# First stage of a hybrid retention and latent-attention step: sample latents in plain float32 column groups, gate weights asked for a tile ahead, gate stores asked for by ScalarE

## The chip, the cores and the metric

The kernel runs on one NeuronCore of one Trainium2 chip. The metric is the device time of one execution in microseconds (us). Instructions of TensorE (PE), VectorE (DVE), ScalarE (ACT), GpSimd (POOL) and SyncE (SP) run in five in-order queues, which wait for each other by semaphores. In the before kernel SP asks for nearly all transfers between HBM and on-chip memory.

## The reference

One inference step of a decoder layer in float32, for 1024 prompt rows and 32 sample rows (8 sequences of 4 tokens), each of 1024 features. Cut to what the change touches:

```
z = rmsnorm(x, ln_w) @ w_in
rq, rk, rv, rg, cq, ckv, kr, mg, ga, gb = split(z)
q   = rmsnorm(cq, q_norm_w) @ w_uq        # cq: 384 columns
ckv = rmsnorm(ckv, kv_norm_w)             # 256 columns
kr  = rope(kr, pos)                       # 64 columns
... retention over (rq, rk, rv), gated by silu(rg)
... paged attention of the sample rows over cached ckv and kr, by a page table; causal attention of the prompt rows; gated by silu(mg)
merged = sigmoid(ga) * h_ret + sigmoid(gb) * h_mla
... output projection, a per-layer embedding, a last norm
```

The change concerns the 704 latent columns (cq, ckv, kr) of the input projection, and its gate columns (ga, gb, rg, mg).

## The kernel before

Float32 products are made from fp32r parts: each operand is split into a high part (a rounded copy, made by ACT or POOL) and a low part (operand less high part, by DVE), and a product is three matmuls, high by high, high by low, low by high (`mac`, L266 to L268). Weights come in by `load_w` and `stage`: SP loads a 128x512 piece into `wr` (two buffers), POOL makes `wh` (L197; later ACT does, L247), DVE makes `wl` (L200).

The first stage treats x in nine tiles in the order `[0, 1, 8, 2, 3, 4, 5, 6, 7]`; tile 8 holds the 32 sample rows. `turn_tile` makes the squares of a tile on ACT (L348, into `xs`), the row norm (`rs_v`, `rs_r`, L233 and L235) on POOL, the transposes on PE (L323, eight of 128x128), copies of them (L324), and stores the turned tile to `xTD`. `scale_tile` spreads the norm over partitions by a matmul (L356), multiplies on DVE (L359, `y`), and makes `xh` on ACT (L364) and `xl` on DVE (L365) for each of eight k blocks. `latent_tile` multiplies a tile by the latent weights (`load_lat`: raw `wlr`, parts `wlh` and `wll`, eight k blocks of 704 columns): 24 matmuls of 384 columns and 24 of 320, whatever the number of rows. Then, twice, squares on ACT (L399), a norm on POOL, a scaling on DVE (L401), the rotation on DVE (L375 to L380), stores, and for prompt rows a block transpose (`lt`, L331) with stores to `latD`. The sample rows' latents stay in `latS`, which `sample_queries` transposes next (L507).

`gate_tiles` is the fill: each gate tile loads one weight tile of 128 columns and runs three thirds of 24 matmuls with 352 columns into one of two `mm` banks; ACT evicts each into `gev` (L417) and SP stores it (L418). `beside` runs the latents of the last three tiles, the sample queries and the page attention with units of that fill between them; what is left runs after. `page_rows` works out the row numbers of the cache pages from the page table; its two tiles, `pt_all` and `own`, lie in the two `xs` buffers. Inside these streams a scheduler places the instructions of each engine, by its own estimates; the order on each engine is then fixed.

## Time and profile before

| | |
|---|---|
| time, three runs | 2135.68, 2136.15, 2139.07 us; median 2136.15 |
| the profiled execution | 2134.45 us; span from first to last instruction 2132.7 |
| granted TensorE clock, mean | 0.998 |
| busy: PE, DVE, ACT, POOL | 2096.1, 1262.0, 723.8, 329.7 us |
| DMA | 316.31 MB, 148 GB/s over the span |

The profile is of one execution. In a timeline a row has the start, the length, the engine, the line, the operation, the tiles written and read, how many are grouped in it, and in square brackets the idle time before it with what ended that. Matmuls are pipelined: a row's length is longer than the step to the next one. SPq rows are the asking for a transfer, not the transfer. In a chain of waits "x <- y: a, b, c" reads: x waited for y, a us in all, b times, the longest c. Names carry no buffer numbers in the profile; in the order of instructions below they do.

### The profile page before, as it was taken

How to read it: one execution, taken by the hardware profiler on the slowest of the kernel's cores; microseconds unless marked ns; L12 is line 12 of the kernel's file. 1: busy time of each engine (PE TensorE's matmuls, PEld its weight loads, DVE VectorE, ACT ScalarE, POOL GpSimd, SP SyncE). 2: the span in 40 equal slices, each digit the busy share in tenths (PEclk: the TensorE clock that was granted, in tenths of full speed). 3: DMA queues.
4: the chain of work that ended last, by engine and by line, in shares of the span. 5: the costliest groups of instructions: out<-in, count | busy, mean ns of one | idle time of the engine just before them, and what ended most of it. 6: DMA issues, size and time to landing. Idle time of an engine off the chain costs nothing. (4 is left out here: it accounts for less than half of the span.)

```text
span 2132.7 us, 38999 instructions
## 1 busy us (share of the span) xinstructions
PE 2096.1 (98%) x15392; PEld 1840.9 (86%) x15392; DVE 1262.0 (59%) x2849; ACT 723.8 (34%) x1541; POOL 329.7 (15%) x522
## 2 busy tenths in 40 slices
PE   8999999999999999999999999999999999999998
PEld 7998777777778897888888887888888999999997
DVE  6535555565655457767676774877777353444465
ACT  5412222333423322222222222454565341222343
POOL 2110111111100022222222220122211000000122
PEclk9999999999999999999999999999999999999999
DMA  7476656566565332754636647210112452333243
GB/s 215 121 218 232 233 192 237 207 246 228 194 237 183 112 75 71 220 147 139 220 72 182 189 139 254 55 46 18 39 56 91 138 192 81 101 87 121 82 143 118
DMA packets 330552, 316.31 MB, mean 148 GB/s; under 512 B 92160, under 2 KB 283840, under 8 KB 326272
## 3 DMA queue, kind: packets, MB, share of 16 engines
q1 hardware_dynamic: 321152, 229.92, 35.8%
q0 software_dynamic: 9216, 83.89, 10.5%
q8 instruction: 121, 1.98, 0.4%
q14 instruction: 63, 0.52, 0.1%
HBM read 245.38 MB, written 68.36 MB: 147 GB/s over the span
## 5 line engine op out<-in xcount | busy, mean ns | idle before, releaser
L266 PE MATMUL mm<-xh,wh 128*128 128x352 f32 x1344 | 455.9, 339 | 0.1
L268 PE MATMUL mm<-xh,wl 128*128 128x352 f32 x1344 | 435.6, 324 | 0.6 <-DVE wl L200 0.6
L267 PE MATMUL mm<-xl,wh 128*128 128x352 f32 x1344 | 435.6, 324 | 0.0
L266 PEld LDWEIGHTS mm<-xh,wh 128*128 128x128 f32 x1344 | 252.4, 188 | 83.3 <-issue 73.3
L267 PEld LDWEIGHTS mm<-xl,wh 128*128 128x128 f32 x1344 | 253.6, 189 | 3.5 <-issue 2.3
L268 PEld LDWEIGHTS mm<-xh,wl 128*128 128x128 f32 x1344 | 253.3, 189 | 3.2 <-issue 1.9
L200 DVE TENSOR_TENSOR wl<-wr,wh 128x512 fp32r<-128x512 f32 (+2 forms) x251 | 176.3, 715 | 119.6 <-ACT wh L247 100.8
L247 ACT CAST wh<-wr 128x512 fp32r<-128x512 f32 x216 | 129.8, 618 | 282.5 <-PE mm L267 254.6
L652 DVE STREAM_TRANSPOSE kt<-craw 128x512 f32<-128x512 f32 x256 | 160.7, 680 | 84.5 <-PE sc L656 79.7
L417 ACT ACTIVATE gev<-mm 128x352 f32<-128x352 f32 x120 | 55.5, 463 | 223.5 <-PE mm L268 141.7
L266 PE MATMUL mm<-mh,wh 128*128 128x352 f32 x384 | 124.6, 324 | 1.4 <-ACT mh L1151 0.8
L267 PE MATMUL mm<-ml,wh 128*128 128x352 f32 x384 | 124.9, 325 | 0.7 <-DVE ml L200 0.6
L268 PE MATMUL mm<-mh,wl 128*128 128x352 f32 x384 | 124.4, 324 | 0.0
L268 PE MATMUL mm<-gh,wl 128*128 128x352 f32 x384 | 124.4, 324 | 0.0
L266 PE MATMUL mm<-gh,wh 128*128 128x352 f32 x384 | 124.4, 324 | 0.0
L267 PE MATMUL mm<-gl,wh 128*128 128x352 f32 x384 | 124.3, 324 | 0.0
L266 PE MATMUL mm<-wv,xh 128*128 128x512 f32 x256 | 103.6, 405 | 0.0
L267 PE MATMUL mm<-wv,xh 128*128 128x512 f32 x256 | 101.0, 395 | 0.0
L268 PE MATMUL mm<-wv,xl 128*128 128x512 f32 x256 | 100.9, 394 | 0.0
L656 PE MATMUL sc<-kt,q 32*32 32x512 f32 x2560 | 91.3, 600 | 0.0
L1580 POOL TENSOR_TENSOR xr<-x1h,x1l 128x352 f32<-128x352 f32 x24 | 27.0, 1146 | 389.1 <-DVE pT L200 311.5
L856 ACT ACTIVATE on<-ac,gb,gs 128x512 f32<-128x512 f32 x36 | 28.0, 778 | 155.1 <-DVE gb L854 150.0
(383 smaller groups left out, 4532.0 us busy)
## 6 DMA issues: line engine op xcount, KB each, us to landing
wr<-in_w_in_dram SPq DMA_DIRECT2D x144, 256.0 KB, 3.6
st<-in_state_ret_dram SPq DMA_DIRECT2D x32, 512.0 KB, 5.3
out_ret_sample_dram<-st SPq DMA_DIRECT2D x32, 512.0 KB, 3.9
wr<-in_w_ple_gate_dram SPq DMA_DIRECT2D x48, 256.0 KB, 2.8
gt<-gev SPq DMA_DIRECT2D x48, 176.0 KB, 3.6
gl<-go SPq DMA_DIRECT2D x16, 528.0 KB, 5.2
gate<-ga SPq DMA_DIRECT2D x16, 528.0 KB, 3.5
g<-gt SPq DMA_DIRECT2D x32, 256.0 KB, 3.2
```

What stands on the lines that cost most here:

```text
L200: dve.tensor_tensor(out=out, in0=src, in1=b32(hi), op=ALU.subtract)
L247: hi_by[0](hi, raw)
L266: pe.matmul(out, wh, xh, start=first, stop=False)
L267: pe.matmul(out, wh, xl, start=False, stop=False)
L268: pe.matmul(out, wl, xh, start=False, stop=last)
L417: act.activation(t, ps, func)
L652: dve.transpose(kt[:, 2 * i + s].rearrange("p (n r) -> p n r", r=32), src)
L656: pe.matmul(sc[32 * v:32 * v + 32, q, :], Q["q4"][qs_, j + v // 2, 2 * (g % 2) + v % 2, :], kt[qs_, v, :], start=n == 0, stop=n == NJ // 2 ...
L856: act.activation(on[:n], po, AF.Identity, bias=nb[:n], scale=s[:n])
L1580: pool.tensor_tensor(out=xr, in0=b32(x1[f][0][:, sl]), in1=b32(x1[f][1][:, sl]), op=ALU.add)
```

## The change

The sample rows leave the ring of tiles. Their x is loaded and turned right behind tile 0, the turned blocks are multiplied by the norm weight on POOL (`xS`, L481, in a `gev` buffer), and 32 plain float32 matmuls, four column groups of 176 for each k block, run on the raw weights `wlr` (now five buffers) between the matmuls of tile 0's first half (L395), into an `mm` bank. At tile 8's place in the ring only the copies out of that bank (four on ACT, L412), the scaling by the row norm on DVE (L413) and the norms remain. `la` has three buffers, `xs` one; `page_rows` takes the `wr` buffers and does its arithmetic two tiles later than its load. `gate_tiles` is one generator over all its groups: it asks for the next weight tile at the fourth of a tile's 24 units, and for the first at the third tile of the ring (`next(fill)`); the fifth merge-gate tile is in the fill itself. The gate stores are asked for by ACT (L440). In the last retention head the fill is cut after 36 units instead of 49.

```diff
@@ -305,11 +305,11 @@
 
     def load_lat(k):
         hi, lo = (p1.tile([P, NLAT], F32R, tag=f"wl{s}{k}", name=f"wl{s}{k}", bufs=1) for s in "hl")
-        raw = p1.tile([P, NLAT], F32, tag="wlr", name="wlr", bufs=4)
+        raw = p1.tile([P, NLAT], F32, tag="wlr", name="wlr", bufs=5)
         sp.dma_start(raw, w_in[k * P:(k + 1) * P, C_LAT:C_LAT + NLAT])
         (hi_pool if k % 2 else act.copy)(hi, raw)
         lo_of(lo, raw, hi)
-        wlat.append((hi, lo))
+        wlat.append((hi, lo, raw))
 
     def turn_input(t, src, dst, nf, by=act.copy):
 
@@ -344,9 +344,13 @@
         n = rows(t)
         xt = xts.pop(t)
         ss = small(p1, "ss")
-        xs = p1.tile([P, D], F32, tag="xs", name="xs", bufs=2)
+        xs = p1.tile([P, D], F32, tag="xs", name="xs", bufs=1)
         act.activation(xs[:n], xt[:n], AF.Square, accum_out=ss[:n])
         r = rstd_of(p1, ss, n, 1.0 / D, dve if t == 0 else pool)
+        if t == 8:
+            r8 = small(p1, "r8", 1, 1)
+            pool.tensor_copy(r8[:n], r[:n])
+            r = r8
         turned[t] = r, turn_input(t, xt, xTD, D // P, dve.tensor_copy if t == 0 else act.copy)
 
     def scale_tile(t):
@@ -384,15 +388,31 @@
     latS = lp.tile([NR, NLAT], F32, name="latS")
     idx = lp.tile([P, NB * NPG // 16], I32, name="idx")
 
+    NG = NLAT // 4
+
+    def sample_latents(k):
+        for r in range(4):
+            pe.matmul(few[0][r * NR:(r + 1) * NR, :NG], few[1][:, k], wlat[k][2][:, r * NG:(r + 1) * NG], start=k == 0, stop=k == 7,
+                      tile_position=(0, r * NR), skip_group_check=True)
+
     def latent_tile(t):
         n = rows(t)
-        pq, pk = ac(), ac()
-        for ps, lo, w in ((pq, 0, QL), (pk, QL, KL + ROPE)):
-            for k in range(8):
-                xk = tuple(v[:, t * P:t * P + n] for v in xn[k])
-                wk = tuple(v[:, lo:lo + w] for v in wlat[k])
-                mac(ps[:n, :w], xk, wk, k == 0, k == 7)
-        la = latS if t == 8 else p1.tile([P, NLAT], F32, tag="la", name="la", bufs=2)
+        if t < 8:
+            pq, pk = ac(), ac()
+            for ps, lo, w in ((pq, 0, QL), (pk, QL, KL + ROPE)):
+                for k in range(8):
+                    xk = tuple(v[:, t * P:t * P + n] for v in xn[k])
+                    wk = tuple(v[:, lo:lo + w] for v in wlat[k][:2])
+                    mac(ps[:n, :w], xk, wk, k == 0, k == 7)
+                    if t == 0 and lo == 0:
+                        sample_latents(k)
+        else:
+            raw = p1.tile([NR, NLAT], F32, tag="la", name="las", bufs=3)
+            for r in range(4):
+                act.activation(raw[:, r * NG:(r + 1) * NG], few[0][r * NR:(r + 1) * NR, :NG], AF.Copy)
+            dve.tensor_scalar(raw, raw, few[2][:NR], None, op0=ALU.mult)
+            pq, pk = raw[:, :QL], raw[:, QL:]
+        la = latS if t == 8 else p1.tile([P, NLAT], F32, tag="la", name="la", bufs=3)
         cq, kv, kr = la[:n, 0:QL], la[:n, QL:QL + KL], la[:n, QL + KL:NLAT].unsqueeze(1)
         for src, dst, w, nw in ((pq[:n, :QL], cq, QL, qnw), (pk[:n, :KL], kv, KL, kvw)):
             ss = small(p1, "ss2")
@@ -408,45 +428,59 @@
             sp.dma_start(O["ckv_sample"].rearrange("l b t c -> (l b t) c"), kv)
             sp.dma_start(O["krope_sample"].rearrange("l b t c -> (l b t) c"), la[:n, QL + KL:])
 
-    def gate_tiles(col, dst, fs, func):
-        for f in fs:
-            w = load_w(w_in[:, col + f * P:col + (f + 1) * P], 8)
-
-            def evac(j, ps, sl, f=f):
+    def gate_tiles(*groups):
+        todo = [(w_in[:, col + f * P:col + (f + 1) * P], dst[f], func) for col, dst, fs, func in groups for f in fs]
+        w = load_w(todo[0][0], 8)
+        yield 0.0
+        for n, (_, dst, func) in enumerate(todo):
+
+            def evac(j, ps, sl, dst=dst, func=func):
                 t = wst.tile([P, TH], F32, tag="gev", name="gev", bufs=2)
                 act.activation(t, ps, func)
-                sp.dma_start(dst[f][:, sl], t)
-            yield from gemm(w, xn, evac, 8)
+                act.dma_start(dst[:, sl], t)
+
+            for i, cost in enumerate(gemm(w, xn, evac, 8)):
+                if i == 3 and n + 1 < len(todo):
+                    w = load_w(todo[n + 1][0], 8)
+                yield cost
 
     def chain(*gs):
         for g_ in gs:
             yield from g_
 
-    fill = chain(gate_tiles(C_GA, gaD, range(8), AF.Copy), gate_tiles(C_GB, gbD, range(8), AF.Copy),
-                 gate_tiles(C_RG, [t[:, f, :] for t in gtD for f in range(4)], range(16), AF.Silu), gate_tiles(C_MG, mgD, range(4), AF.Silu))
+    fill = gate_tiles((C_GA, gaD, range(8), AF.Copy), (C_GB, gbD, range(8), AF.Copy),
+                      (C_RG, [t[:, f, :] for t in gtD for f in range(4)], range(16), AF.Silu), (C_MG, mgD, range(5), AF.Silu))
 
     def page_rows():
-        pt_all = p1.tile([P, NB * NPG], I32, tag="xs", name="pt_all", bufs=2)
+        pt_all = wst.tile([P, NB * NPG], I32, tag="wr", name="pt_all", bufs=2)
         sp.dma_start(pt_all, A["page_table"].rearrange("b n -> (b n)").unsqueeze(0).to_broadcast([P, NB * NPG]))
-        own = p1.tile([P, NB * NPG], F32, tag="xs", name="own", bufs=2)
+        yield
+        own = wst.tile([P, NB * NPG], F32, tag="wr", name="own", bufs=2)
         dve.tensor_copy(own, pt_all)
         own = own.rearrange("p (i g) -> p i g", g=16)
         dve.tensor_tensor(out=own, in0=own, in1=C("page").unsqueeze(1).to_broadcast([P, NB * NPG // 16, 16]), op=ALU.mult)
         row = small(p1, "row", NB * NPG // 16, 1)
         dve.tensor_reduce(out=row, in_=own, axis=AX.X, op=ALU.add)
         dve.tensor_scalar(idx, row, C("mod"), None, op0=ALU.add)
+        yield
 
     head = at["maskT"][0]
     load_x(0)
     sp.dma_start(cst[:, :head], A["consts"][:, :head])
     sp.dma_start(lnw, A["ln_w"][0].rearrange("(f p) -> p f", p=P))
+    load_x(8)
     turn_tile(0)
     scale_tile(0)
     order = [0, 1, 8, 2, 3, 4, 5, 6, 7]
-    for k in range(8):
+    load_lat(0)
+    load_x(1)
+    turn_tile(8)
+    few = [mm(), wst.tile([P, 8, NR], F32, tag="gev", name="xS", bufs=2), turned[8][0]]
+    for half, st in enumerate(turned[8][1]):
+        fs = slice(4 * half, 4 * half + 4)
+        pool.tensor_tensor(out=few[1][:, fs], in0=st[:, :, :NR], in1=lnw[:, fs].unsqueeze(2).to_broadcast([P, 4, NR]), op=ALU.mult)
+    for k in range(1, 8):
         load_lat(k)
-        if k % 4 == 0:
-            load_x(order[1 + k // 4])
     sp.dma_start(qnw, A["q_norm_w"][0:1, :].to_broadcast([P, QL]))
     sp.dma_start(kvw, A["kv_norm_w"][0:1, :].to_broadcast([P, KL]))
     sp.dma_start(ropeM, A["ropeM"])
@@ -455,21 +489,22 @@
     load_x(order[3])
 
     def latents():
+        table = page_rows()
         for n, t in enumerate(order):
             if n + 4 < 9:
                 load_x(order[n + 4])
             if 0 < n < 7:
                 turn_tile(order[n + 2])
             latent_tile(t)
-            if n == 0:
-                turn_tile(order[2])
             if n < 7:
                 scale_tile(order[n + 2])
             if n == 1:
                 sp.dma_start(cst[:, head:], A["consts"][:, head:at["turn"][0]])
                 sp.dma_start(gnw, A["ret_gn_w"][0].rearrange("(f p) -> p f", p=P))
-            if n == 4:
-                page_rows()
+            if n in (4, 6):
+                next(table)
+            if n == 2:
+                next(fill)
             yield 7.1 if n > 5 else 0.0
 
     beside(latents(), 3 * 7.1, fill, 36)
@@ -759,7 +794,6 @@
     gph.close()
     open_banks()
     run(fill)
-    run(gate_tiles(C_MG, mgD, range(4, 5), AF.Silu))
     ph.close()
     lph.close()
 
@@ -1124,8 +1158,8 @@
             def early(cost):
                 first_w.extend(rope_weights(0))
                 yield cost
-            gates = gate_tiles(C_MG, mgD, range(5, 8), AF.Silu)
-            rest = (chain(islice(gates, 49), early(0.0), gates), 31.8)
+            gates = gate_tiles((C_MG, mgD, range(5, 8), AF.Silu))
+            rest = (chain(islice(gates, 36), early(0.0), gates), 31.8)
         run(woven((chain(chunks, sample_state(h, X)), 27.9 if h + 1 < HR else 32.4), rest))
         X = nxt
     hi_by[0] = hi_pool
```

**PE at tile 0.** What stood in its row before, from the start of the latents (`xh_112` and `xl_113` to `xh_126` and `xl_127` are the parts of the eight k blocks of the turned x, `wlh` and `wll` those of the weights; L356 is the scale matmul):

```order
L266 MATMUL ac<-wlh_187,xh_112 128x384
L267 MATMUL ac<-wll_188,xh_112 128x384
L266 MATMUL ac<-wlh_187,xh_112 128x320
L267 MATMUL ac<-wll_188,xh_112 128x320
L268 MATMUL ac<-wlh_187,xl_113 128x384
L266 MATMUL ac<-wlh_195,xh_114 128x384
L267 MATMUL ac<-wll_196,xh_114 128x384
L268 MATMUL ac<-wlh_195,xl_115 128x384
L268 MATMUL ac<-wlh_187,xl_113 128x320
```

and now:

```order
L323 MATMUL tr<-cst,xt 128x32 x8
L395 MATMUL mm<-wlr,xS 32x176 x4
L323 MATMUL tr<-cst,xt 128x128 x8
L266 MATMUL ac<-wlh_189,xh_112 128x384
L266 MATMUL ac<-wlh_189,xh_112 128x320
L267 MATMUL ac<-wll_190,xh_112 128x384
L268 MATMUL ac<-wlh_189,xl_113 128x384
L267 MATMUL ac<-wll_190,xh_112 128x320
L268 MATMUL ac<-wlh_189,xl_113 128x320
L360 MATMUL tr<-cst,rs_r_276 128x128
L360 MATMUL tr<-cst,r_204 128x32
L395 MATMUL mm<-wlr,xS 32x176 x4
```

The turned sample tile and its first four float32 matmuls stand ahead of tile 1's transposes and of the first latent; further groups follow between the latents.

**SP at the start.** Before:

```order
L303 DMA xt<-in_x_prompt_dram 128x1024
L441 DMA cst<-in_consts_dram 128x129
L442 DMA lnw<-in_ln_w_dram 128x8x1
L309 DMA wlr<-in_w_in_dram 128x704
L303 DMA xt<-in_x_prompt_dram 128x1024
L309 DMA wlr<-in_w_in_dram 128x704
L325 DMA xTD<-turn 128x4x128 x2
L309 DMA wlr<-in_w_in_dram 128x704 x3
L303 DMA xt<-in_x_sample_dram 32x1024
L309 DMA wlr<-in_w_in_dram 128x704 x3
```

and now:

```order
L303 DMA xt<-in_x_prompt_dram 128x1024
L469 DMA cst<-in_consts_dram 128x129
L470 DMA lnw<-in_ln_w_dram 128x8x1
L303 DMA xt<-in_x_sample_dram 32x1024
L309 DMA wlr<-in_w_in_dram 128x704
L303 DMA xt<-in_x_prompt_dram 128x1024
L325 DMA xTD<-turn 128x4x128 x2
L325 DMA xTD<-turn 128x4x32 x2
L309 DMA wlr<-in_w_in_dram 128x704 x7
```

The sample rows are loaded third, and the second to eighth weight tile stand behind the four stores of turned tiles 0 and 8.

**POOL at the end of the ring.** The last norms of tiles 6 and 7 (two each) and the gate weights, before:

```order
L233 TENSOR_SCALAR rs_v_1354<-ss_1352 128x1
L235 TENSOR_TENSOR rs_r_1356<-rs_v_1354,cst 128x1
L233 TENSOR_SCALAR rs_v_1361<-ss_1359 128x1
L235 TENSOR_TENSOR rs_r_1363<-rs_v_1361,cst 128x1
L197 TENSOR_SCALAR wh<-wr 128x512 x5
L233 TENSOR_SCALAR rs_v_1538<-ss_1536 128x1
L235 TENSOR_TENSOR rs_r_1540<-rs_v_1538,cst 128x1
L197 TENSOR_SCALAR wh<-wr 128x512
L233 TENSOR_SCALAR rs_v_1545<-ss_1543 128x1
L235 TENSOR_TENSOR rs_r_1547<-rs_v_1545,cst 128x1
```

and now:

```order
L233 TENSOR_SCALAR rs_v_1358<-ss_1356 128x1
L235 TENSOR_TENSOR rs_r_1360<-rs_v_1358,cst 128x1
L233 TENSOR_SCALAR rs_v_1365<-ss_1363 128x1
L235 TENSOR_TENSOR rs_r_1367<-rs_v_1365,cst 128x1
L233 TENSOR_SCALAR rs_v_1542<-ss_1540 128x1
L235 TENSOR_TENSOR rs_r_1544<-rs_v_1542,cst 128x1
L233 TENSOR_SCALAR rs_v_1549<-ss_1547 128x1
L235 TENSOR_TENSOR rs_r_1551<-rs_v_1549,cst 128x1
L197 TENSOR_SCALAR wh<-wr 128x512 x6
```

Before, five weight pieces stand ahead of tile 7's norms and one between them; now all six stand behind them.

**PE at the same place.** The last of tile 7's latents (`ac<-`) and what follows (`mm<-` is gate work), before:

```order
L268 MATMUL ac<-wlh_227,xl_125 128x320
L266 MATMUL ac<-wlh_233,xh_126 128x320
L267 MATMUL ac<-wll_234,xh_126 128x320
L268 MATMUL ac<-wlh_233,xl_127 128x320
L266 MATMUL mm<-xh_126,wh 128x352
L267 MATMUL mm<-xl_127,wh 128x352
L268 MATMUL mm<-xh_126,wl 128x352
L266 MATMUL mm<-xh_112,wh 128x352
L267 MATMUL mm<-xl_113,wh 128x352
```

and now, where L542 and L543 transpose `latS`:

```order
L266 MATMUL ac<-wlh_262,xh_126 128x320
L267 MATMUL ac<-wll_263,xh_126 128x320
L268 MATMUL ac<-wlh_262,xl_127 128x320
L542 MATMUL tr<-cst,latS 128x32 x5
L543 MATMUL tr<-cst,latS 64x32
L266 MATMUL mm<-xh_112,wh 128x352
L267 MATMUL mm<-xl_113,wh 128x352
L268 MATMUL mm<-xh_112,wl 128x352
L266 MATMUL mm<-xh_114,wh 128x352
```

Before, gate work of loaded weights follows the latents; now the transposes follow, and then the first matmul of the gate tile whose `wh` stands last in POOL's row above.

**DVE at the same place.** Tile 7's second half, before:

```order
L200 TENSOR_TENSOR wl<-wr,wh 128x512
L401 SCALAR_TENSOR_TENSOR la<-ac,rs_r_1547,kvw 128x256
L375 TENSOR_TENSOR kro_1550<-ac,ropeM 128x32
L376 TENSOR_TENSOR kro_1551<-ac,ropeM 128x32
L377 TENSOR_TENSOR la<-kro_1550,kro_1551 128x32
L378 TENSOR_TENSOR kro_1550<-ac,ropeM 128x32
L379 TENSOR_TENSOR kro_1551<-ac,ropeM 128x32
L380 TENSOR_TENSOR la<-kro_1550,kro_1551 128x32
L331 STREAM_TRANSPOSE lt<-la 128x704
L200 TENSOR_TENSOR wl<-wr,wh 128x512 x2
```

and now:

```order
L421 SCALAR_TENSOR_TENSOR la<-ac,rs_r_1551,kvw 128x256
L379 TENSOR_TENSOR kro_1554<-ac,ropeM 128x32
L380 TENSOR_TENSOR kro_1555<-ac,ropeM 128x32
L381 TENSOR_TENSOR la<-kro_1554,kro_1555 128x32
L382 TENSOR_TENSOR kro_1554<-ac,ropeM 128x32
L383 TENSOR_TENSOR kro_1555<-ac,ropeM 128x32
L384 TENSOR_TENSOR la<-kro_1554,kro_1555 128x32
L331 STREAM_TRANSPOSE lt<-la 128x704
L200 TENSOR_TENSOR wl<-wr,wh 128x512 x6
```

The low parts of six weight pieces now stand behind tile 7's rotation and block transpose.

## Prediction

> **What bounds the kernel now.** I read the page first, then the chain of waits of TensorE in the first 110 us, then timelines of the few places that it names.
>
> ```profile
> PE 2096.1 (98%) x15392; PEld 1840.9 (86%) x15392; DVE 1262.0 (59%) x2849; ACT 723.8 (34%) x1541; POOL 329.7 (15%) x522
> ...
> PE tr L356 <- POOL rs_r L235: 7.2, 4, 3.3
> ...
> PE mm L268 <- DVE wl L200: 0.6, 1, 0.6
> ```
>
> TensorE is busy for 98% of the span, so only two things move the time here: TensorE work that goes away, and holes in TensorE's row. The last two rows (the waits of TensorE from 0 to 110 us: total, times, longest) name nearly all the holes that this change can touch: 7.2 us in four waits of the scale matmul for a row norm, and one wait for gate weights. The windows from 107 to 800 us have but that last wait (their sum, length and then each engine's busy time):
>
> ```profile
> sum 693.00, PE 692.41 PEld 564.06 DVE 363.53 ACT 215.75 POOL 84.80; mean PE 138.48 PEld 112.81 DVE 72.71 ACT 43.15 POOL 16.96
> ```
>
> So the time is decided before 130 us. The profiled execution took 2134.45 us (1.75 of it outside the span of 2132.7), 1.70 under the median of 2136.15; I sum differences and apply them to the median.
>
> **Part 1: tile 8 as float32 groups beside tile 0.** The sample rows' own turn on TensorE disappears. It ran here:
>
> ```profile
> 12.32 0.67 PE L266 MATMUL ac<-wlh,xh 128*128 128x384 f32 x1
> ...
> 19.82 0.68 PE L323 MATMUL tr<-cst,xt 32*128 32x32 f32 x8
> 20.43 0.44 PE L268 MATMUL ac<-wlh,xl 128*128 128x384 f32 x1
> ...
> 25.21 0.38 ACT L399 ACTIVATE la<-ac 128x256 f32<-128x256 f32 x1
> 27.94 0.40 PE L356 MATMUL tr<-cst,rs_r 32*128 32x32 f32 x2 [1.91 <-POOL rs_r L235]
> 28.27 0.45 PE L267 MATMUL ac<-wll,xh 128*128 128x384 f32 x1
> ...
> 34.03 0.31 PE L268 MATMUL ac<-wlh,xl 128*128 128x320 f32 x1
> 34.18 0.38 PE L356 MATMUL tr<-cst,rs_r 128*128 128x128 f32 x2
> ...
> 43.11 0.42 PE L266 MATMUL ac<-wlh,xh 128*128 128x384 f32 x1
> ```
>
> Tiles 0 and 1 end at 34.18; tile 2 begins at 43.11, 8.93 us later, most of it tile 8's 48 matmuls, which take as long with 32 rows as with 128.
>
> What replaces them are 32 float32 matmuls with a 128x32 stationary block and 176 columns: the first four ahead of tile 0's latents, the other 28 in eight runs (4, 4, 1, 3, 1, 7, 1, 7) between full-width matmuls. The trace has that shape at 384 columns, and one longer run of 256 columns:
>
> ```profile
> 147.72 0.84 PE L528 MATMUL mm<-early 128*32 128x384 f32 x4
> 148.70 0.43 PE L266 MATMUL mm<-xh,wh 128*128 128x352 f32 x1
> 148.96 0.32 PE L267 MATMUL mm<-xl,wh 128*128 128x352 f32 x1
> 149.12 0.32 PE L268 MATMUL mm<-xh,wl 128*128 128x352 f32 x1
> ...
> 152.44 2.12 PE L528 MATMUL mm<-early 128*32 128x384 f32 x18
> 154.49 0.43 PE L267 MATMUL mm<-xl,wh 128*128 128x352 f32 x1
> ...
> 217.00 3.66 PE L687 MATMUL x<-craw,pT 128*32 128x256 f32 x64
> ```
>
> A run of 4 takes 0.98 us start to start, one of 18 takes 2.05: 0.076 each, so 0.67 of the first is fixed. The step behind it (148.70 to 148.96) is 0.26 where the next (to 149.12) is 0.16: a seam of 0.10, and I count as much ahead of a run. Scaled from 384 to 176 columns, seams unscaled, a run costs 0.20 + 0.67 x 0.458 = 0.51 and each matmul 0.035: 8 x 0.51 + 28 x 0.035 = 5.0 us. Unscaled it is 8 x 0.87 + 28 x 0.076 = 9.1; at the long run's rate (3.66 / 64 = 0.057) with seams alone 28 x 0.057 + 8 x 0.20 = 3.2. I take 5.0, from the row of the same stationary block, and keep 3.2 and 9.1. The Trainium skill speaks against the change here: TensorEngine Tiling (Array Packing), Key Properties, says that "Mode switching requires drain", so each run would empty the array twice. A drain as long as what a record outlasts its step (0.32 less 0.16) would make the 16 seams 2.6 us instead of 1.6 and the time 2133.8; the trace's seam rows are 0.10, and I stay with them.
>
> Up to the end of tile 1 the sum is: groups +5.0; the hole at 27.94 goes with tile 8's place, -1.9; tile 8's small transposes (19.58 to 20.43 between neighbouring matmuls) move into the idle start, -0.8; two scale matmuls move from there behind the first latents, +0.3; the slow clock of the start (below) overlaps with the groups, -0.6 (0 to -1.2). The start itself shifts:
>
> ```profile
> 3.22 0.43 SPq L309 DMA_DIRECT2D wlr<-in_w_in_dram  x1
> 6.56 1.23 SPq L325 DMA_DIRECT2D xTD<-turn  x2
> 7.84 1.52 SPq L309 DMA_DIRECT2D wlr<-in_w_in_dram  x3
> 7.28 0.80 PE L356 MATMUL tr<-cst,rs_r 128*128 128x128 f32 x2 [0.62 <-POOL rs_r L235]
> 8.57 1.94 PE L323 MATMUL tr<-cst,xt 128*128 128x128 f32 x8 [0.49 <-DVE wll L200]
> ```
>
> The scale of tile 0 at 7.28, tile 8's transposes behind it to about 9.2, xS at 9.6, the first float32 run (0.98 above; 1.3 allowed for the slow clock), tile 1's transposes (1.94): the first latent at 12.85 instead of 12.32, +0.5. SP now asks for weight tiles 1 to 7 behind four stores of turned tiles; tile 8's wait for its copies until about 9.5, so the second weight tile, asked for at 3.22 before, comes some 7 us later. TensorE has the eight runs and wider work to fill that, so I add nothing, but keep +1.5 for the upper end. Sum to tile 1's end: +2.5, at 36.7.
>
> Then tile 2. Its scale and tile 3's now stand right behind tile 1. On POOL tile 3's norm stands behind both norms of tile 1's latents, as tile 8's did at 27.94: 2.73 us from the ACT row at 25.21 to the scale at 27.94, and 0.33 more to the next matmul. So tile 2 begins 3.1 us behind tile 1's end, at 39.8, and loses some 0.7 to tile 1's block transpose, which stands between tile 3's xl pieces on DVE. 39.8 + 0.7 against 43.11: **-2.7 us**, between -4.8 and +2.9. The four copies of sample PSUM on ACT and the scaling on DVE lie beside tile 1's and 2's matmuls, which need neither: 0.
>
> **Part 2: page_rows gives xs back.**
>
> ```profile
> 71.31 0.43 DVE L432 CAST own<-pt_all 128x512 f32<-128x512 int32 x1 [3.77 <-DMA pt_all<-in_page_table_dram]
> 74.54 1.05 ACT L348 ACTIVATE xs<-xt 128x1024 f32<-128x1024 f32 x1
> 76.57 1.58 POOL L235 TENSOR_TENSOR rs_r<-rs_v,cst 128x1 f32<-128x1 f32 x3
> 77.18 0.49 PE L356 MATMUL tr<-cst,rs_r 128*128 128x128 f32 x2 [3.28 <-POOL rs_r L235]
> 78.34 0.51 PE L266 MATMUL ac<-wlh,xh 128*128 128x320 f32 x1
> 81.85 0.35 PE L267 MATMUL ac<-wll,xh 128*128 128x320 f32 x1
> ```
>
> The page table fills both xs buffers, so the squares of tiles 6 and 7 wait until it has been read, the norms for the squares and the scale for the norms: 3.28 us. Behind it 13 matmuls take 3.51 us (78.34 to 81.85) where the step at full clock is 0.15 (34.03 to 34.18): 13 x 0.15 = 1.95, so 1.6 us of slow clock. The page table moves to the weight buffers and its arithmetic two tiles later; one xs buffer is enough, since the squares run one behind another on ACT. **-4.9 us.** What is late next are the scales of tiles 5 and 6: their norms wait for the same squares, which now run as soon as their x tile is there.
>
> **Part 3: gate weights a tile ahead.** The wait of 0.6 us at 107.45 goes, **-0.6**. But the order of the changed kernel shows a new one. Gate tile 1's halves are rounded on POOL behind tile 7's last norm, and their low part on DVE behind tile 7's rope and block transpose, while TensorE has put tiles 6 and 7 ahead of that gate tile and has then only six small transposes in hand. Before, the same chain had other latents over it:
>
> ```profile
> 103.25 0.31 PE L268 MATMUL ac<-wlh,xl 128*128 128x320 f32 x1
> 103.65 0.38 ACT L399 ACTIVATE la<-ac 128x256 f32<-128x256 f32 x1 [6.42 <-PE ac L268]
> 105.01 1.20 POOL L197 TENSOR_SCALAR wh<-wr 128x512 fp32r<-128x512 f32 x2
> 106.71 0.69 DVE L200 TENSOR_TENSOR wl<-wr,wh 128x512 fp32r<-128x512 f32 x1
> 107.31 0.91 DVE L331 STREAM_TRANSPOSE lt<-la 128x704 f32<-128x704 f32 x1
> ...
> 140.26 0.49 PE L507 MATMUL tr<-cst,latS 32*128 32x32 f32 x5
> ```
>
> Laid over the new order: last latent at 103.25, the small transposes (0.49 for five, with their seams) done 0.7 later, first wh at 105.6, so a hole of 1.7; two matmuls to 106.0; the block transpose from 106.71 (0.83), then wl (0.74) to 108.28, a hole of 2.3. **+4.0**, between 0 (nothing waits) and 4.0, and up to 1.6 of slow clock behind it, as behind the 3.28 hole; behind the 1.9 hole at 27.94 one matmul alone was slow. I take half, **+0.8**. The Trainium skill (TensorE: Matmul & The Clock Gate, Part 1) has the clock halve after an idle window of about 3.4 us whose phase runs free; by it two holes of 1.7 and 2.3 cost nothing, 2132.0, unless the pair counts as one, 2133.6. The trace's hole of 3.28 is already short of that window and was followed by a slow clock, so it doesn't decide.
>
> **Part 4: gate stores from ACT.**
>
> ```profile
> L667 ACT COPY sums<-sc 64x1024 f32<-64x1024 f32 x32 | 32.4, 1011 | 71.5 <-PE sc L656 59.5 <-DVE nm L668 11.8
> ...
> L417 ACT ACTIVATE gev<-mm x120: 453/464/471, 93.2 to 1330.7; 128x352 f32<-128x352 f32 x120
> L418 SPq DMA_DIRECT2D ga<-gev x24: 319/338/3406, 93.7 to 224.2; - x24
> ```
>
> Each of 120 stores (minimum, median, maximum in ns) now takes 0.34 us of ACT's queue, and casts, evictions and softmax pieces wait behind it. A third of a gate tile is 24 matmuls of 0.16, 3.9 us, and there is a second bank: an eviction may be that late. ACT is idle for 477 of the 693 us summed above. I take 0; the cover gone, 120 x 0.34 = +41. The shorter opening in the last retention head and the folded last gate tile move no work: 0.
>
> **Sum.** -2.7 - 4.9 - 0.6 + 4.0 + 0.8 = -3.4: 2132.8 us (2131.0 for the profiled execution).
>
> **The rivals.**
> - The new wait of part 3 is covered, because TensorE is later than I lay it or the weights are rounded sooner: 2132.8 - 4.8 = 2128.0. Against it stands the fixed order on POOL. Chance 0.20.
> - The groups cost 9.1 instead of 5.0, by seams or by waiting for raw weights that now come behind four stores: 2136.9, no change. For it: one-matmul runs, each tied to a transfer's end. 0.20.
> - The page-table hole stays, because its steps now wait for a weight buffer: 2132.8 + 4.9 = 2137.7. The arithmetic is two tiles later, which speaks against it. 0.08.
> - Slower: ACT held by stores. Its longest issue before was 3.41 us; with a copy of sums (1.01) and the eviction itself (0.46) behind it a bank comes free after 4.9 us, 1.0 past the 3.9. From eight such places (2140.8) the kernel is slower by what can be told; twelve give 2145. 0.12.
>
> **How the numbers follow.** My case has 0.40, half of it faster by more than 0.2% (4.3 us, about what a measurement of this kernel tells from no change), since it lies 3.4 under the median. With the rivals: faster 0.20 + 0.20 = 0.40; same 0.20 + 0.19 + 0.06 = 0.45; slower 0.12 + 0.03 = 0.15. The range goes from 2126 (first rival, groups at 3.2) to 2138 (second and third); only the last rival is outside. The likeliest case alone has 2130 to 2136.
>
> **What would show it.** After: tile 2's latents near 40; no hole over 1 us between 60 and 85 and no slow matmuls there; a hole of TensorE for wh, then one for wl, where tile 7 ends; float32 runs of about half a microsecond each; no hole from 150 to 800. I am wrong if that last hole is missing, if the first weights hold TensorE before 25 us, or if holes behind ACT's stores show.

## The result, and the profile after

The changed kernel takes 2131.23 us (median of 20 runs, 2127.97 to 2135.08) against 2134.70 us of the kernel before (20 runs, the first three among them): ratio 0.9979, 95% interval 0.9972 to 0.9985, so 0.21% or about 4.5 us faster. The forecast was 2132.8 us. The profiled execution took 2129.97 us, with a span of 2128.2 against 2132.7 before.

The page of the changed kernel, its first lines:

```profile
span 2128.2 us, 38977 instructions
...
PE 2091.2 (98%) x15408; PEld 1835.8 (86%) x15408; DVE 1261.7 (59%) x2850; ACT 723.2 (34%) x1543; POOL 333.1 (16%) x527
```

TensorE is busy 4.9 us less, and still for 98%. Of the waits of TensorE in the changed kernel from 0 to 135 us, these matter here (what waited, for what; total, times, longest):

```profile
PE tr L360 <- POOL rs_r L235: 2.8, 3, 1.2
PE mm L268 <- DVE wl L200: 2.1, 1, 2.1
PE mm L266 <- POOL wh L197: 1.6, 1, 1.6
```

The four waits of the scale matmul (now L360) for a norm, 7.2 us before, are three of 2.8 us in all. Two waits for gate weights, 2.1 and 1.6 us, have come in. Where the first tiles end, in the timeline of the changed kernel's TensorE:

```profile
4.79 1.94 PE L323 MATMUL tr<-cst,xt 128*128 128x128 f32 x8 [4.79 <-DMA cst<-in_consts_dram]
...
14.57 0.51 PE L395 MATMUL mm<-wlr,xS 128*32 128x176 f32 x8
15.00 0.59 PE L266 MATMUL ac<-wlh,xh 128*128 128x384 f32 x2
...
19.31 0.49 PE L395 MATMUL mm<-wlr,xS 128*32 128x176 f32 x2
19.72 0.44 PE L267 MATMUL ac<-wll,xh 128*128 128x384 f32 x1
...
20.45 0.80 PE L395 MATMUL mm<-wlr,xS 128*32 128x176 f32 x14
21.17 0.41 PE L266 MATMUL ac<-wlh,xh 128*128 128x320 f32 x1
...
36.16 0.38 PE L360 MATMUL tr<-cst,rs_r 128*128 128x128 f32 x2
...
38.58 0.49 PE L360 MATMUL tr<-cst,rs_r 128*128 128x128 f32 x2 [1.16 <-POOL rs_r L235]
38.82 0.42 PE L266 MATMUL ac<-wlh,xh 128*128 128x384 f32 x1
```

A float32 matmul leaves two records (the 32 leave 64), so x2 is a run of one, x8 of four and x14 of seven: 0.41, 0.43 and 0.72 us from the start to the next instruction. Four take hardly longer than one. They lie in four column groups, and in the trace their first records start within 0.02 us of each other (14.57 to 14.59): they run side by side. Seven are two such sets, of three and of four. Tile 1 ends at 36.16, where tile 2's scale stands; the scale of tile 3 waits 1.16 us behind it, and tile 2's latents begin at 38.82. Before they began at 43.11. From there to tile 7's end:

```profile
66.24 0.49 PE L360 MATMUL tr<-cst,rs_r 128*128 128x128 f32 x2 [1.04 <-POOL rs_r L235]
...
102.42 0.49 PE L542 MATMUL tr<-cst,latS 32*128 32x32 f32 x5
103.36 0.55 POOL L235 TENSOR_TENSOR rs_r<-rs_v,cst 128x1 f32<-128x1 f32 x1
103.89 1.20 POOL L197 TENSOR_SCALAR wh<-wr 128x512 fp32r<-128x512 f32 x2
104.56 0.43 PE L266 MATMUL mm<-xh,wh 128*128 128x352 f32 x1 [1.61 <-POOL wh L197]
105.71 0.91 DVE L331 STREAM_TRANSPOSE lt<-la 128x704 f32<-128x704 f32 x1
106.54 1.25 DVE L200 TENSOR_TENSOR wl<-wr,wh 128x512 fp32r<-128x512 f32 x2
107.25 0.66 PE L268 MATMUL mm<-xh,wl 128*128 128x352 f32 x1 [2.10 <-DVE wl L200]
...
112.69 0.40 PE L268 MATMUL mm<-xh,wl 128*128 128x352 f32 x1
112.94 0.32 PE L266 MATMUL mm<-xh,wh 128*128 128x352 f32 x1
113.10 0.33 PE L267 MATMUL mm<-xl,wh 128*128 128x352 f32 x1
```

The scale of tile 6, which stands ahead of tile 5's latents, still waits, 1.04 us. At tile 7's end the rounding of gate weights on POOL stands behind tile 7's norm, and their low part on DVE behind its block transpose: holes of 1.61 and 2.10 us. Behind them 18 matmuls go from 107.25 to 112.69, 0.30 each where the next step is 0.16: 5.44 - 18 x 0.16 = 2.5 us of slow clock. The window from 100 to 120 us (core's time, busy times of PE, PEld, DVE, ACT, POOL, then the granted clock) shows it, 0.83:

```profile
100.00:120.00 20.00, 16.29 (x89) 15.69 (x88) 6.53 (x14) 1.40 (x4) 4.15 (x7) 0.83 0.52 115
```

Last, the queries of the sample rows, and what ACT does behind them:

```profile
144.57 2.14 PE L563 MATMUL mm<-early 128*32 128x384 f32 x24
146.10 0.62 ACT L247 CAST wh<-wr 128x512 fp32r<-128x512 f32 x1 [4.85 <-DMA ga<-gev]
147.23 0.40 PE L266 MATMUL mm<-xh,wh 128*128 128x352 f32 x1 [0.52 <-ACT gev L439]
```

Their 12 float32 matmuls, three sets of four column groups, stood in runs of two, one and nine before (0.98, 0.76 and 2.05 us: 3.79 us) and are one run of 2.14 now. The hole of 0.52 behind it waits for an eviction (`gev`), which stands on ACT behind a weight cast; that cast had itself waited, by the profile for a gate store to land.

Laid together, changed against before: tile 2's start -4.3; the page-table hole -3.3 and the slow clock behind it -1.6; the scale of tile 6 +1.0; the former wait for `wl` -0.6; the two new holes +3.7; the slow clock behind them +2.5; the sample queries -1.65; the hole behind them +0.5. That is -3.75 of the span's -4.5; the remaining -0.75 is not placed.

### The profile page after: what moved, and what is told of

The parts are those of the page before. It is cut to its first block, busy times and chain, and to the rows that moved or that the text cites. A ratio compares the mean times of both kernels' runs of the same rounds, so it can differ in the third digit from the quotient of the medians.

```text
span 2128.2 us, 38977 instructions
## 1 busy us (share of the span) xinstructions
PE 2091.2 (98%) x15408; PEld 1835.8 (86%) x15408; DVE 1261.7 (59%) x2850; ACT 723.2 (34%) x1543; POOL 333.1 (16%) x527
```

## The experiments

Times of different chips differ by some 10 us (the kernel before took 2134.7 to 2144.1), so each kernel is given by its ratio to the kernel before on its own chip, with the 95% interval. Differences between kernels of different chips rest on these ratios. The changed kernel run once more, the two-tiles-ahead kernel and the two with weight tiles asked for sooner ran on chips on which the kernel before takes 2136.0 and 2136.6 us. All others ran on two chips on which it takes 2144.1 and 2143.8; the changed kernel itself was not run there. That its ratio is near 0.998 on these too is assumed below, not shown; the two kernels nearest to it came to 0.9975 and 0.9970 there. The changed kernel run once more came to 2131.14 us:

> The changed kernel unaltered, on the chip of these runs, as the measure for the others. Expected: ratio to the kernel before 0.998, as first measured, with the holes of 1.6 and 2.1 us at tile 7's end. Rival: on this chip, on which the kernel before takes some 9 us more, the ratio is nearer 1, and the comparisons of the earlier experiments with 0.998 were against the wrong number.

Ratio 0.9981 (0.9972 to 0.9991): the result stands, with the same holes (1.61 and 2.10). The rival, another ratio on a slower chip, was not put to the test: the kernel before took 2136.03 here. The slow clock behind them was shorter in this execution. Its first slow matmul and the first one at full speed again:

```profile
107.89 0.44 PE L267 MATMUL mm<-xl,wh 128*128 128x352 f32 x1
...
111.36 0.33 PE L267 MATMUL mm<-xl,wh 128*128 128x352 f32 x1
```

These 12 steps take 3.47 us, 1.5 more than at 0.16 each; 2.5 was one execution's value.

**The page table alone, in the kernel before** (`page_rows` in the `wr` buffers, its arithmetic two tiles later, one `xs`).

```diff
-        pt_all = p1.tile([P, NB * NPG], I32, tag="xs", name="pt_all", bufs=2)
+        pt_all = wst.tile([P, NB * NPG], I32, tag="wr", name="pt_all", bufs=2)
...
-            if n == 4:
-                page_rows()
+            if n in (4, 6):
+                next(table)
```

> The kernel before with one part of the change: the page table in the weight buffers, its arithmetic two tiles later, one xs buffer. In the order of this kernel the gate weights stand behind tile 7's last norm on GpSimd, as in the changed kernel, though nothing is asked for ahead. Theory: the wait of TensorE where tile 7 ends comes from this part, because once the page table stalls nobody the scheduler runs the latents of tiles 6 and 7 through and places the gate weights behind them. Then the 3.3 us hole near 74 and the slow matmuls behind it are gone (-4.9), but holes of about 1.6 and 2.1 us for wh and wl stand where tile 7 ends, with some 2.5 us of slow clock behind: -4.9 - 0.6 + 3.7 + 2.5, within 1.5 us of the kernel before. Rival (the prediction's part 3): the wait comes with the weights asked for ahead. Then no hole over 1 us at tile 7's end and about 5 us faster than before.

Ratio 0.9989 (0.9980 to 0.9998). TensorE's holes from 20 to 110 us:

```profile
28.40 0.40 PE L356 MATMUL tr<-cst,rs_r 32*128 32x32 f32 x2 [1.91 <-POOL rs_r L235]
97.48 0.43 PE L266 MATMUL mm<-xh,wh 128*128 128x352 f32 x1 [2.13 <-POOL wh L197]
100.17 0.66 PE L268 MATMUL mm<-xh,wl 128*128 128x352 f32 x1 [2.10 <-DVE wl L200]
```

The hole of 3.28 us is gone, and the two holes at tile 7's end are there, without any asking ahead. So the new wait belongs to part 2. With the page table out of the way the scheduler places the work at the ring's end in another order, and the gate weights land behind tile 7's norms. The sample queries are one run of 2.14 us in this kernel too, and behind them stands a hole of 1.18 us for an eviction. Summed up, its rows make it some 0.7 us slower than the kernel before (with 2.4 us of slow clock behind the two holes); its ratio says 2.4 us faster, give or take 2. The difference is not placed.

**No asking ahead** (the changed kernel with each gate tile's load at its own begin, the cut at 49 units again).

```diff
-        w = load_w(todo[0][0], 8)
-        yield 0.0
...
+            yield from gemm(load_w(todo[n][0], 8), xn, evac, 8)
...
-            if n == 2:
-                next(fill)
...
```

> The changed kernel, with each gate tile's weights asked for when that tile begins, as before. Theory (the order of tiles 6 and 7 makes the wait, not the asking ahead): holes for wh and wl at tile 7's end stay, at 1.5 and 2 us or more, since even the first gate tile's weights are now rounded behind tile 7's norm; time within 2 us of the changed kernel. Rival (asking ahead makes the wait): hole at most 0.6 us, 5 to 6 us faster than the changed kernel.

Ratio 0.9975 (0.9966 to 0.9984), not to be told from the changed kernel. Its holes at tile 7's end:

```profile
94.69 0.66 PE L266 MATMUL mm<-xh,wh 128*128 128x352 f32 x1 [2.06 <-POOL wh L197]
97.79 0.66 PE L268 MATMUL mm<-xh,wl 128*128 128x352 f32 x1 [2.15 <-DVE wl L200]
```

Both remain, 2.06 and 2.15. Asking ahead neither makes these holes nor gives a gain that can be told.

**Sample rows back in the ring** (the changed kernel with tile 8 as 48 fp32r matmuls at its former place, and the loads of the start in their former order).

```diff
...
-        if t < 8:
-            pq, pk = ac(), ac()
...
-                    if t == 0 and lo == 0:
-                        sample_latents(k)
-        else:
...
+        pq, pk = ac(), ac()
...
```

> The changed kernel with the sample rows back in the ring of tiles as 48 full matmuls of 32 rows; page table, gate weights and stores as changed. Theory: the plain float32 groups are worth 4.3 us (tile 2 begins at 38.8 instead of 43.1), so tile 2 begins near 43 here, the hole of 1.9 us ahead of the sample rows' scale is back, and the time is about 4 us over the changed kernel, no faster than the kernel before. Rival (the groups cost what they save, and the gain comes from the page table's part): within 1 us of the changed kernel.

Ratio 1.0008 (0.9999 to 1.0017): some 6 us slower than the changed kernel, and no gain is left. Part of it is a hole at another place. TensorE and ACT there:

```profile
154.64 0.62 ACT L247 CAST wh<-wr 128x512 fp32r<-128x512 f32 x1 [7.90 <-DMA wr<-in_w_in_dram]
155.17 0.46 ACT L419 ACTIVATE gev<-mm 128x352 f32<-128x352 f32 x1
...
155.77 0.63 PE L266 MATMUL mm<-xh,wh 128*128 128x352 f32 x1 [4.48 <-ACT gev L419]
```

An eviction stands on ACT behind a cast whose weights come late, and TensorE waits 4.48 us for the bank; the changed kernel has 0.52 there, 1.44 when run again. So 3 to 4 us come from this hole. The rest is the ring itself: with the same gate work done, the hole for `wh` at tile 7's end is over 104.3 us after the first transposes, 99.8 in the changed kernel and 100.2 and 100.4 in two others on chips of 2144 (the two kernels with other gate stores below). So the groups in place of tile 8's turn are worth about 4 us there. The two make 7 to 8 together, and the ratio, loose by some 2 us, says 6.

**Less fill beside the ring**, so that gate work is not exhausted where tile 7 ends.

```diff
-    beside(latents(), 3 * 7.1, fill, 36)
+    beside(latents(), 3 * 7.1, fill, 9)
```

> The changed kernel with one number: the gate work run beside the last three tiles has a budget of 9 instead of 36. In its order seven gate units of the first gate tile stand behind tile 7's latents, and three more behind the small transposes: 30 matmuls of 0.16, 4.9 us, where the chain to wh takes 2.4 and to wl 5.0. Theory: both holes (1.6 and 2.1) and the slow clock behind them (2.5) go: about 6 us faster than the changed kernel, near 2125. Rival: the wait only moves to where that gate tile ends, or the work moved out of the ring costs the same later: within 2 us of the changed kernel.

Ratio 1.0020 (1.0011 to 1.0029), slower:

```profile
108.02 0.43 PE L266 MATMUL mm<-xh,wh 128*128 128x352 f32 x1 [3.24 <-POOL wh L197]
...
127.75 1.46 PE L563 MATMUL mm<-early 128*32 128x384 f32 x2 [9.77 <-DVE kt L687]
```

The `wl` hole is gone, the `wh` hole is twice as long (the weights are asked for only at 103.56), and TensorE waits 9.77 us ahead of the sample queries. The profile puts that to a transpose on DVE; the queries' weights, asked for from 118.20 on, are as likely, since the next matmul waits for them again. The wait was moved, not removed.

**Fill kept for the last tile** (page table in the `wlr` buffers, the three units of fill time given 1.5, 1.5 and 18.3 us instead of 7.1 each).

```diff
-        pt_all = wst.tile([P, NB * NPG], I32, tag="wr", name="pt_all", bufs=2)
+        pt_all = p1.tile([P, NB * NPG], I32, tag="wlr", name="pt_all", bufs=5)
...
-            yield 7.1 if n > 5 else 0.0
+            yield (0.0, 1.5, 21.3 - 2 * 1.5)[max(n - 5, 0) and (1 if n < 8 else 2)]
```

> The changed kernel with two edits: the page table lies in two of the raw latent weights' buffers (free by then) instead of the gate weights', and the gate work beside the last three tiles keeps its total but is dealt out late: 12 units before tile 7's latents, the rest behind them. In its order 36 gate matmuls (5.8 us) and the small transposes (0.7) stand behind tile 7's latents and ahead of the first that needs weights rounded behind tile 7's norm (2.4 us to wh, 5.0 to wl), and the gate work done by the time of the sample queries is the same as in the changed kernel, which the smaller budget had not kept. Theory: no hole over 0.5 us where tile 7 ends, no slow clock behind it, none of 9.8 us in the sample queries: 1.6 + 2.1 + 2.5 = 6.2 us faster than the changed kernel, about 0.5% faster than the kernel before. Rival: the weights for that gate tile come late whatever the order (as in the run with less fill, 3.2 us), or the wait comes back where the next gate tile begins: within 2 us of the changed kernel.

Ratio 0.9970 (0.9959 to 0.9981, from 7 runs); it overlaps with the changed kernel's interval. TensorE's first hole (one of 2.14 us for `wh` follows at 134.86), and the waits of SP's queue from 60 to 130 us:

```profile
106.56 0.43 PE L266 MATMUL mm<-xh,wh 128*128 128x352 f32 x1 [3.52 <-POOL wh L197]
```

```profile
SPq L333 <- DMA ga<-gev: 28.7, 4, 15.1
```

SP's stores of `latD` wait 28.7 us in four waits for the landing of gate stores that ACT asked for, and the loads of gate weights stand behind them in SP's queue.

**Two gate tiles' weights ahead**, the second asked for at the ring's fourth tile, on top of the last edit.

```diff
+        ahead = load_w(todo[1][0], 8)
+        yield 0.0
...
-            if n == 2:
+            if n in (2, 3):
                 next(fill)
```

> As the late fill, and the second gate tile's weights are asked for at the fourth tile of the ring too, so both tiles' weights are rounded long before tile 7's last norm; 108 gate matmuls (17.5 us) stand behind tile 7's latents and wait for nothing of it. In the late fill the gate tile's weights had been late by 3.5 us because SyncE, ahead of asking for them, waited for the landing of gate stores that ScalarE asks for (28.7 us in four waits). Theory: with the weights asked for before those stores, no hole over 0.5 us between 68 and 125 us and no slow clock there: 5 to 6 us faster than the changed kernel on the same chip (next run). Rival: the ring is followed by another wait of the same size (for the third gate tile's weights or for the sample queries' w_uq, both still behind tile 7's stores on SyncE): holes of 2 us or more between 125 and 155 us, and within 2 us of the changed kernel.

Ratio 0.9992 (0.9983 to 1.0000). The holes at tile 7's end are gone; a longer one stands behind them:

```profile
123.03 0.66 PE L266 MATMUL mm<-xh,wh 128*128 128x352 f32 x1 [8.37 <-POOL wh L197]
```

```profile
SPq L333 <- DMA ga<-gev: 19.7, 3, 14.3
SPq L424 <- DMA ga<-gev: 11.6, 2, 9.3
```

Again SP waits for ACT's gate stores, 31.3 us in these two rows, and the third tile's weights come late.

**Gate stores asked for by SP again** (changed kernel).

```diff
-                act.dma_start(dst[:, sl], t)
+                sp.dma_start(dst[:, sl], t)
```

> The changed kernel with the gate stores asked for by SyncE again. Theory: 120 issues of 0.33 us on ScalarE lie in its idle time and hold nobody, so the time stays within 1.5 us of the changed kernel, and the holes of TensorE up to 130 us stay as they are. Rival: evictions are late behind ScalarE's stores: then the holes behind evictions between 130 and 800 us (0.5 us in the changed kernel) go and it is 2 us or more faster. Other rival: the stores on SyncE held up its weight loads: then it is 2 us or more slower than the changed kernel.

Ratio 1.0010 (1.0001 to 1.0019), about 0.3% or 6 to 7 us slower than the changed kernel:

```profile
149.54 2.12 PE L563 MATMUL mm<-early 128*32 128x384 f32 x18 [2.85 <-DMA early<-in_w_uq_dram]
```

The holes at tile 7's end are unaltered (1.62, 2.10); 2.85 us of new waiting are for the weights of the sample queries, which SP now asks for behind gate stores. The remaining 3 to 4 us are not placed.

**Every gate store in two halves, both asked for by ACT.**

```diff
-                act.dma_start(dst[:, sl], t)
+                act.dma_start(dst[:64, sl], t[:64])
+                act.dma_start(dst[64:, sl], t[64:])
```

> The changed kernel with each gate store split in two halves of 64 partitions, both asked for by ScalarE: 120 more issues, some 40 us more of ScalarE's queue. Theory (ScalarE has the room): within 1.5 us of the changed kernel. Rival (stores on ScalarE press on evictions): slower than the changed kernel by several us, with holes behind evictions between 130 and 800 us.

Ratio 0.9994 (0.9985 to 1.0003). By the medians of the ratios the 120 further asks cost some 3 us, 0.03 each and not 0.34; the intervals of the two kernels touch, so the size is loose.

**Only four of the 32 float32 matmuls** (each of the four now begins and ends its own sum; the sample rows' latents are then not computed).

```diff
...
-                    if t == 0 and lo == 0:
+                    if t == 0 and lo == 0 and k == 0:
```

> The changed kernel with only the first four of the 32 plain float32 sample matmuls; the other 28 are left out, so the sample rows' values aren't computed. It prices these 28. Theory: TensorE is bound by its own work there, so the eight runs with their seams give back what they take in the changed kernel's trace, 4.2 us plus 1.4 of seams: tile 2 begins near 33.3 instead of 38.8, 5 us or more faster than the changed kernel. Rival: the weights, now behind four stores, are what TensorE runs behind, and the runs fill its waits: holes for weights appear before 25 us and it is less than 3 us faster.

Ratio 1.0000 (0.9991 to 1.0009): with less work, not faster than the changed kernel but some 4 us slower. Its TensorE:

```profile
33.14 0.38 PE L360 MATMUL tr<-cst,rs_r 128*128 128x128 f32 x2
...
36.41 0.44 PE L266 MATMUL ac<-wlh,xh 128*128 128x384 f32 x1 [2.01 <-ACT xh L368]
...
61.46 0.49 PE L360 MATMUL tr<-cst,rs_r 128*128 128x128 f32 x2 [2.33 <-POOL rs_r L235]
...
83.62 0.49 PE L360 MATMUL tr<-cst,rs_r 128*128 128x128 f32 x2 [1.20 <-POOL rs_r L235]
```

Tile 1 ends 3.0 us sooner (33.14 against 36.16), not the 5 that the expectation had: the slow steps of the start (0.27 to 0.32 us a matmul) reach to 18.6 instead of about 14, and TensorE waits 0.21 us for a low weight part. Then the ring waits for `xh` and for norms, 5.5 us in these three holes and 6.7 with two small ones behind the first two, where the changed kernel has 2.2 (1.16 and 1.04). Behind the hole of 2.33, 13 matmuls go at 0.26 us instead of 0.15, 1.5 us more. With the same work done, the hole for `wh` at tile 7's end is over 103.7 us after the first transposes, 3.9 later than in the changed kernel. The ring is paced by what prepares the tiles, and work taken away ahead of it comes back as waiting, here with more on top.

**Two weight tiles asked for ahead of the turned tiles' stores**, first with the two-tiles-ahead edit, then alone on the changed kernel.

```diff
     load_lat(0)
     load_x(1)
+    load_lat(1)
+    load_lat(2)
     turn_tile(8)
...
```

> As e9_two_ahead, and the second and third latent weight tile are asked for before the sample rows' turned tiles are stored, as SyncE's order before the change had them. Theory (TensorE is bound by its own work there): tile 2 begins within 0.5 us of where it does without this edit, and the time is the same within 1 us. Rival (late weights make tile 0's latents wait, and the float32 runs only fill that wait): tile 2 begins 1 us or more earlier.

> The changed kernel with one edit: the second and third latent weight tile are asked for ahead of the sample rows' stores. In the run before this one, tile 2's scale came 2.0 us sooner behind the first transposes with that edit, and the hole at the scale of tile 5 shrank from 1.04 to 0.17. Theory (the late weights cost the start some 2 us: the float32 runs and the latents of tile 0 had waited in their place): tile 2's scale near 36.8 instead of 38.6, no hole over 0.3 at tile 5's scale, the holes of 1.6 and 2.1 at tile 7's end unchanged, 2 to 3 us faster than the changed kernel, ratio to the kernel before 0.997. Rival (the 2 us are given back at the next waits, as when 28 matmuls were left out): within 1 us of the changed kernel, ratio 0.998.

Ratios 0.9980 (0.9971 to 0.9989) with the two-tiles-ahead edit and 0.9980 (0.9971 to 0.9989) alone. The starts, first of the edit alone, then of the changed kernel run again:

```profile
4.72 1.51 PE L323 MATMUL tr<-cst,xt 128*128 128x128 f32 x6 [4.72 <-DMA cst<-in_consts_dram]
...
37.61 0.49 PE L360 MATMUL tr<-cst,rs_r 128*128 128x128 f32 x2 [1.16 <-POOL rs_r L235]
...
79.54 0.49 PE L360 MATMUL tr<-cst,rs_r 128*128 128x128 f32 x2 [1.18 <-POOL rs_r L235]
```

```profile
5.12 1.30 PE L323 MATMUL tr<-cst,xt 128*128 128x128 f32 x5 [5.12 <-DMA cst<-in_consts_dram]
...
38.79 0.49 PE L360 MATMUL tr<-cst,rs_r 128*128 128x128 f32 x2 [1.16 <-POOL rs_r L235]
```

Measured from the first transposes, the scale ahead of tile 2's latents (tile 3's; the expectation calls it tile 2's) comes 0.8 us sooner (32.89 against 33.67). The hole at the scale of tile 6 is gone, one of 1.18 us at the scale of tile 7 (79.54) has come, and the hole for `wh` at tile 7's end is over within 0.1 us of the changed kernel. With the two-tiles-ahead edit the same scale came 2.0 us sooner, and a hole of 7.99 us stood at 120.42; why 2.0 there and 0.8 here is not placed. Behind the sample queries the kernel with the edit alone has a hole of 1.88 us, and a slow stretch that begins at the fifth matmul behind it and lasts to 151.58:

```profile
147.39 0.40 PE L266 MATMUL mm<-xh,wh 128*128 128x352 f32 x1 [1.88 <-ACT gev L439]
...
148.39 0.50 PE L268 MATMUL mm<-xh,wl 128*128 128x352 f32 x1
...
151.58 0.32 PE L267 MATMUL mm<-xl,wh 128*128 128x352 f32 x1
```

The steps between the last two rows are 11 of 0.29 us, where full speed is 0.16. No version tried is faster than the changed kernel by what can be told.

## Why the prediction was right, and where only by its sum

The time (2132.8 forecast, 2131.2 measured) and the sum of differences (-3.4; -3.5 by the medians, -4.5 by the ratio) agree. Of its steps some hold, and others miss by 1 to 2 us in both directions: that they cancel is luck.

- **Part 1, float32 groups.** Priced -2.7, measured -4.3. The groups were put at 5.0; the eight runs measure 4.2 from their starts to the next instruction, 5.6 with a seam of 0.1 on either side. The price came near by luck, for its rows were misread: they count records, two to a matmul, so the run "of 4" has two matmuls and the one "of 18" nine, and its own formula would have given 6.0. Nor does a matmul have a price of its own: up to four, in different column groups, take the time of one. The first latent came at 11.91 instead of 12.85, and tile 1's end at 36.16 instead of 36.7; tile 2 follows after 2.66 instead of 3.1. The step that failed is the 0.7 for `xl` behind tile 1's block transpose: no such hole is there. Weights behind four stores were priced at nothing, +1.5 at most: asking for two of them sooner moves tile 2 by 0.8 us (2.0 in the other kernel) and the time by nothing that can be told.
- **Part 2, page table.** The -4.9 came as worked out. Of the scales that the prediction named as late next, that of tile 6 is a hole of 1.04 us; it had no price, and by the prediction's own sign no hole over 1 us was to stand between 60 and 85.
- **Part 3, the new wait.** Its place and size are right, 1.7 and 2.3 forecast, 1.61 and 2.10 measured, from the order and the rows alone. Its cause is wrong: the order of the whole change was read, and the wait was put to the part that touches gate weights. The page table's edit alone makes it, and without asking ahead it stays. The net worth of part 2 is thus about what that kernel shows, 0.11%, not 4.9 us.
- **The slow clock behind it** is the term that was mis-sized: 0.8, half of 1.6, against 2.5 in the profiled execution and 1.5 in a second. The Trainium skill (TensorE: Matmul & The Clock Gate, Part 1) lets the clock halve after an idle window of about 3.4 us. The runs differ from it, and neither of the prediction's two readings covers them: a single hole of 1.88 us was followed by 11 slow matmuls, one of 3.28 by 13, the pair by 10 to 18 in nine executions, and single holes of 1.44 and 1.91 by one at most. How idle time is counted stays open.
- **Part 4, ACT's stores.** Priced at nothing, since they only leave SP. Giving them back to SP costs about 0.3% by the ratios. One wait of 2.85 us for weights that SP then asks for later is seen; the rest is not placed. That term was missing, and it is the larger side; the cost on ACT is small, as forecast. SP still waits for these stores in the changed kernel: its ask for the store of a turned tile stands 14.6 us, by the profile until a gate store has landed. A sign of being wrong shows in a small form, the 0.52 us hole behind `gev` (1.44 when run again, 4.48 in the kernel with the sample rows in the ring). It comes from a weight cast ahead of the eviction. What held the cast is by the profile a gate store in the changed kernel and the weights themselves in the other; the page table's kernel, whose stores SP asks for, has 1.18 there. So ACT's stores are not excluded as a part of it.
- **Not foreseen:** the sample queries in one run, -1.65, and the hole behind them. The prediction did not look at how float32 runs of unchanged code would be grouped. The page table's edit alone groups them so.

The rival that the new wait is covered would have needed another order on POOL; the one that groups cost 9.1, the page hole's and the slower one are refuted by the rows above. What stays open is a version without a wait at tile 7's end: the two that removed both holes there got one of 8.37 and of 7.99 us behind it, after SP had waited some 30 us for the landing of ACT's stores. Why an ask of SP waits for a store that shares no tile with it the profile does not show, and stores with completion signals of their own were not tried.

## What to carry to other kernels

Where one engine is busy for 98% and a scheduler sets the order, an edit that removes a wait also re-places the work behind it: build each part alone and read its order before a new wait is put to one of them. Work or waiting taken away ahead of a paced ring returns at the ring's next norm (with 28 matmuls left out, 3.0 us saved, and then 4.5 us more of holes and 1.5 of slow clock), so price a gain at the last place that it must pass. When stores move to another engine's queue, count what their old queue can now ask for sooner, and what there still waits for their landing.

## What the runs showed of the hardware

- Two holes of 1.61 and 2.10 us with two matmuls between them were followed by 5.4 us of slow clock (0.30 us a matmul against 0.16), 3.5 us in another execution. Single holes differ: 11 slow matmuls behind one of 1.88 us, 13 behind one of 3.28, at most one behind 1.44 and 1.91.
- Float32 matmuls with 32 columns of weights in four column groups run side by side: with 176 columns a run of one, three or four takes 0.41 to 0.44 us (one took 0.63), of seven 0.72. A run of 12 with 384 columns takes 2.14 us; as runs of two, one and nine they took 3.79.
- SP's asks can wait, by the profile, for transfers that ACT asked for: up to 15.1 us in one wait.
- The same kernel took 2134.7 to 2144.1 us on the chips of these runs (0.4%), and the changed kernel's ratio came out alike in its two comparisons (0.9979 and 0.9981), where the kernel before took 2134.7 and 2136.0.
